# Attention blended five steps to four with the gate projections, 22 dense matmuls taken from the second RWKV inverse, 20 put between the third quarter's masks, and the merge released behind them

## The chip, the cores and the metric

One core of a Trainium2 chip runs the whole layer in one launch. The metric is the device time of that launch in microseconds; lower is better. TensorE (PE) does the matmuls and the 128x128 transposes, VectorE (DVE) and ScalarE (ACT) the elementwise work, GpSimd (POOL) a few powers and some DMA issues, and the SyncE queue (SP) issues most DMAs, in order.

## The reference

A decoder layer over 1024 tokens of width 1024, in float32. What matters here:

```python
p_rwkv, p_att, p_idx, p_gate = jnp.split(rmsnorm(h, norm1_g) @ w_in, c, axis=-1)
y_a = rwkv7_mix(token_shift(p_rwkv, tshift_mu), ...)      # a scan over tokens, 8 heads of 64x64 state
y_b = dsa_attention(q, k, v, q_idx, k_idx, w_idx)         # each query attends to its 256 best keys
g_a, g_b = jnp.split(jax.nn.sigmoid(p_gate), 2, axis=-1)
merged = g_a * (y_a @ w_o_rwkv) + g_b * (y_b @ w_o_att)
h = h + merged @ w_out
z_gate, z_up = jnp.split(rmsnorm(h, norm2_g) @ w_ffn_in, 2, axis=-1)
h = h + (jax.nn.silu(z_gate) * z_up) @ w_ffn_out
return rmsnorm(h, normf_g)
```

## The kernel before

The tokens are two halves of 512 (half 0 and half 1). Every dense projection is three matmul passes per 128x128 weight tile (`mm3`, lines 142, 143 and 147): weights and activations are split into a rounded high part and a remainder, and high x high, high x low and low x high are added up in one PSUM bank `acc`, 24 matmuls of 128x512 for an inner width of 1024. These are the **dense** matmuls below. Everything else of TensorE goes through five PSUM banks called `mix`.

RWKV is worked in four **quarters** of 256 tokens (`q` = 0 to 3; the page's quarter names below are "first" to "fourth"), two in each call of `rwkv`. A quarter has a chain of small steps that can't be dense: the decay matmuls (line 573), the norms of k (sums at line 603, transposes at 626, a power on POOL, transposes at 638, spreading at 646), the **masks** (line 701: for each of four chunks eight small matmuls of B/K against A/R into two `mix` banks, which DVE multiplies with a causal mask into `MT`, line 705, and whose diagonal blocks SP stores to `d_n`, line 712), the transposes of B/K into `NAT` (line 720), the **inverse** of 64 triangular 32x32 blocks (SP loads `N` from `d_n`, line 730; DVE runs 31 steps, lines 739 and 741; SP stores `d_w` and loads `TT`, lines 743 and 752; DVE transposes `TZ`, line 755), and then the chunk steps, which begin at line 769.

Between these steps PE is given other work from a queue `fill` of generators. Each generator issues a few matmuls and yields how many; `pump(n)` adds n credits and draws from the queue until they are used up, and `ticks(n, m)` does it in m portions, with one step of a top-k search beside each. PE's instructions run in exactly the order in which the code issues them; on the other engines and in the DMA queues a scheduler sets the order. In the first three quarters the queue holds: v's projection, the gates of half 0, and then `att0`, which draws 16 steps of the gates of half 1 and then blends the attention of half 0 with the rest of these gates.

A step of a gate yields 4 matmuls. An attention unit (head pair and query block) is five steps: logits of one head (line 1097), transposes of the unit before (line 1132), the same for the second head, and the values of the unit before that (line 1142); a finished head pair has its sums spread (line 1157). The logits are biased and reduced on DVE (line 1099) and made exponentials on ACT (line 1102); the transposes are copied out by ACT (line 1134).

`ready` is called once, in the third quarter. It draws everything that is left in the queue, gives the memory of attention and of the activations of half 1 (`u1hi`, `u1lo`) free, and begins the **merge** of half 0: SP loads the two branches' outputs, 8 tiles of 128x512 (line 1267), into `ylo`, ACT rounds each into `yhi` (line 116) and DVE takes the difference (line 117). `ylo` and `yhi` lie where `u1lo` and `u1hi` lay, so the loads wait for the last matmul that reads `u1lo`, the rounding for the last that reads `u1hi`. Then the merge's dense matmuls and the feed-forward of half 0 are the fill of the rest of RWKV.

Of the kernel before, what the change touches and what calls it, by code (L numbers as in the profile page):

```python
# [51 lines left out]
def block_kernel(ctx: ExitStack, tc: tile.TileContext, ins: dict, outT: bass.AP, outR: bass.AP, stop=None, dbg=None):  # L52
# [56 lines left out]
    def mix():  # L109
        return psM.tile([128, HT], F32, tag="mix", name="mix")  # L110
# [66 lines left out]
    def pump(n):  # L177

        credit[0] += n
        while credit[0] > 0 and fill:  # L180
            try:
                credit[0] -= abs(next(fill[0]))
            except StopIteration:
                fill.popleft()
        if not fill:
            credit[0] = 0
# [3 lines left out]
    def ticks(n, m):  # L190

        for i in range(m):
            pump(n * (i + 1) // m - n * i // m)
            next(beside[0], None)

    def run(*gens):
        for g in gens:
            for _ in g:
                pass
# [7 lines left out]
    def blend(a, b, n, m):  # L207

        a, b = iter(a), iter(b)
        while a is not None or b is not None:  # L210
            for _ in range(n):
                if a is not None:
                    y = next(a, None)
                    if y is None:
                        a = None
                    else:
                        yield y
            for _ in range(m):
                if b is not None:
                    y = next(b, None)  # L220
                    if y is None:
                        b = None
                    else:
                        yield y
# [6 lines left out]
    def opened(side, name, **kw):  # L231
        stack = ExitStack()
        return stack, stack.enter_context(tc.tile_pool(name=name, bufs=1, side=side, reuse_waits="tile", **kw))
# [272 lines left out]
    def proj_gates(half, u, tiles):  # L506
        for g in tiles:

            def out(_, ps):
                t = tmp()  # L510
                V.tensor_tensor(t, ps, rows[half], op=ALU.mult)
                A.activation(t, t, AF.Tanh, scale=0.5)
                A.dma_start(d_g[half][g], t)

            yield from proj(CT_GA + g, [u], out)
# [27 lines left out]
    def rwkv(half, p, consts, ready=None):  # L543
# [5 lines left out]
        for q in range(2 * half, 2 * half + 2):  # L549
# [135 lines left out]
            for e in range(2):  # L685
                SY.dma_start(d_bs[q][e], bs[e::32, :])

            if q == 2:
                ready()


            MT = []
            for c in range(4):
                pr, pa = divmod(c, 2)
                m = p.tile([128, 8, 128], F32, tag=f"x{c}", name="MT")
                pss = [mix(), mix()]
                for hh in range(4):
                    for g in range(2):
                        h = 2 * hh + g
                        ct, ro = h // 2, slice((h % 2) * 64, (h % 2) * 64 + 64)  # L700
                        T.matmul(pss[g][:, hh * 128:(hh + 1) * 128],
                                 BK[ct // 2][ro, ct % 2, pr, 2 * pa:2 * pa + 2, :].rearrange("p s t -> p (s t)"),
                                 AR[ro, ct, c, :, :].rearrange("p s t -> p (s t)"), start=True, stop=True)
                for g in range(2):
                    V.tensor_tensor(m[:, g::2, :], pss[g].rearrange("p (h t) -> p h t", h=4),
                                    cmask[:, 64 - 64 * pa:192 - 64 * pa].unsqueeze(1).to_broadcast([128, 4, 128]),
                                    op=ALU.mult)
                MT.append(m)
                ba = 64 - 64 * pa
                for b in range(2):  # L710
                    i0 = (c * 2 + b) * 8
                    SY.dma_start(d_n[q][i0:i0 + 8].rearrange("h s t -> s h t"),
                                 m[ba + 32 * b:ba + 32 * b + 32, :, ba + 32 * b:ba + 32 * b + 32])
            NAT = []
            for pr in range(2):
                n = p.tile([128, 2, 512], F32, tag=f"x{4 + pr}", name="NAT")
                for pa in range(2):
                    ps = mix()
                    for ct in range(4):
                        T.transpose(ps[:, ct * 128:(ct + 1) * 128],  # L720
                                    BK[ct // 2][:, ct % 2, pr, 2 * pa:2 * pa + 2, :].rearrange("p s t -> p (s t)"),
                                    ident)
                    A.activation(n[:, pa, :], ps, AF.Copy)
                NAT.append(n)

# [32 lines left out]
                             d_bs[q][e].rearrange("c s -> (c s)").partition_broadcast(64))  # L760
            bon = v
            G.tensor_tensor(bon, v, bsp, op=ALU.mult)
            ticks((211, 236, 281, 232)[q], (13, 4, 10, 6)[q])
            both = [(h, pa, 64 - 64 * pa, 64 * pa) for h in range(8) for pa in range(2)]
            hd = [(h, h // 2, slice((h % 2) * 64, (h % 2) * 64 + 64), slice(h * 64, h * 64 + 64)) for h in range(8)]
            for pr in range(2):
# [54 lines left out]
            for pr in range(2):  # L821
                yb = p.tile([128, 2, 512], F32, tag=("P", "x6")[pr], name="yb")
                yc, y2 = yb[:, 0, :], yb[:, 1, :]
                for pa in range(2):
# [35 lines left out]
                    for h, ct, ro, hc in hd:  # L860
                        pp = at[ct % 2][0]
                        T.matmul(ps[ro, ct * 64:ct * 64 + 64], NAT[pr][:, pp, hc], UV[pr][:, pp, hc],
                                 start=True, stop=True)
# [45 lines left out]
    def masks(bp, p):  # L909

        caus = p.tile([128, 128], F32, name="caus")
        bias, kept = {}, {}
        for b in range(8):
            n = (b + 1) * 128
            if b in LATE:
                kept[b] = bp.tile([128, n], F32, name=f"kept{b}")
                bias[b] = kept[b].bitcast(BF16)[:, 0:n]
            else:
                bias[b] = bp.tile([128, n], BF16, name=f"bias{b}")
            if b < 2:  # L920
                V.memset(bias[b], 0.0)
        bp.tile([128, 16], F32, name="edge")
        return caus, bias, kept
# [560 lines left out]
    def ffn(half, zp, zs, kept):  # L1484

        for gi in range(len(GROUPS)):
            f = act_tiles(zp, "f", ("s2", "s0"))
            yield from ffn_in(f, zs, gi)
            if gi < len(GROUPS) - 1:
                yield from ffn_out(half, zp, f, gi)  # L1490
        kept.append(f)
# [165 lines left out]
    def chain(*gens):  # L1657
        for g in gens:
            yield from g
# [10 lines left out]
    caus, bias, kept = masks(bp, cp2)  # L1670
# [33 lines left out]
    at0 = []  # L1704

    def att0():
        spj.close()
        su.pop().close()
        at0.append(opened("right", "at0"))
        gates = proj_gates(1, us[1], range(16))  # L1710
        for _ in range(16):
            yield next(gates)
        yield from blend(attend(0, at0[0][1], bias), gates, 2, 2)

    fill.append(att0())
    rwkv(0, rp, consts)
    zps, z0, f0 = [], [], []

    def ready():

        run(*fill)
        fill.clear()
        at0[0][0].close()
        su.pop().close()
        zps.append(opened("left", "zp0"))
        m = merge(0, zps[0][1], z0)
        next(m)
        fill.append(chain(m, ffn(0, zps[0][1], z0, f0)))

    rwkv(1, rp, consts, ready)  # L1730
    wq[0] = SY
    sz0, zp0 = zps[0]
# [114 lines left out]
```

## Time and profile before

| | us |
|---|---|
| runs | 1724.02, 1715.69, 1714.16 |
| median | 1715.69 |
| profiled execution | 1717.53 |
| its span in the trace | 1715.5 |
| PE busy | 1686.8 (98% of the span) |
| DVE, ACT, POOL busy | 1187.7, 893.5, 94.8 |

A row of a timeline gives start, length, engine, line, operation, output and input, count, and in brackets the idle time before it with what ended it. In the count a matmul of two plain float32 operands that the code issues once may stand as two, so the 32 mask matmuls of a quarter are 64 there. A row of the stages gives the length of the stretch, then for PE, PE's weight loads, DVE, ACT and POOL the busy time, then the granted clock of TensorE (1.00 is full speed), the DMA engines' share and GB/s.

### The profile page before, as it was taken

The numbers are of one execution on the slowest core, as the hardware profiler recorded it, in microseconds if no ns is written. First come the engines' busy times: TensorE is split into PE (matmuls) and PEld (weight loads), VectorE is DVE, ScalarE is ACT, GpSimd is POOL, SyncE is SP. The second block draws the span as 40 slices with busy tenths as digits, with TensorE's granted clock in tenths as the row PEclk, the third lists the DMA queues.
The fourth block names the chain that finished last, engine by engine and source line by source line (L and its number), as shares of the span: only waits on it lengthen the run. The fifth ranks groups of instructions, "written<-read, shape, count | busy, mean of one in ns | idle before, by whom it ended". The sixth has DMA issues, their size and how long they took to land.

```text
span 1715.5 us, 28185 instructions
## 1 busy us (share of the span) xinstructions
PE 1686.8 (98%) x10748; PEld 1417.2 (83%) x10748; DVE 1187.7 (69%) x2314; ACT 893.5 (52%) x1720; POOL 94.8 (6%) x107
## 2 busy tenths in 40 slices
PE   8999999999999998999999999999999999999998
PEld 6888888878778776878787888878888899899998
DVE  6789989966467558867885655535564896686763
ACT  6365898453544688755324365533323454353442
POOL 0000000000021110000100110000000000000002
PEclk9999999999999999999999999999999999999999
DMA  5452334446357625663342633245456344635532
GB/s 214 161 153 86 99 107 151 135 114 168 104 166 209 179 90 161 193 190 109 92 123 88 232 117 120 73 155 173 138 187 182 115 156 137 183 91 148 168 112 99
DMA packets 141944, 243.58 MB, mean 142 GB/s; under 512 B 48833, under 2 KB 71041, under 8 KB 141681
## 3 DMA queue, kind: packets, MB, share of 16 engines
q1 hardware_dynamic: 119072, 170.76, 32.6%
q10 hardware_dynamic: 16128, 48.60, 9.1%
q0 software_dynamic: 6608, 22.42, 4.3%
q8 instruction: 85, 1.39, 0.3%
q14 instruction: 51, 0.41, 0.1%
HBM read 188.73 MB, written 53.00 MB: 141 GB/s over the span
## 4 chain that ended last, share of the span: by engine, by line
PE 62%; DVE 4%; ACT 2%; issue 1%; DMA 1%; POOL 1%; SPq 0%; ACTq 0%; POOLq 0%; DVEq 0%
PE acc L142 13%; PE acc L147 12%; PE acc L143 12%; PE acc L160 3%; PE mix L1557 2%; PE mix L1555 2%; PE mix L1554 2%; PE mix L1142 2%; PE mix L1132 2%; PE mix L1116 1%; PE acc L1557 1%; PE acc L1554 1%; PE acc L1555 1%; DVE wlo L117 1%; PE mix L831 1%
## 5 line engine op out<-in xcount | busy, mean ns | idle before, releaser
L117 DVE TENSOR_TENSOR wlo<-wst,whi 128x1024 fp32r<-128x1024 f32 (+1 forms) x204 | 248.2, 1218 | 179.3 <-PE acc L147 71.6
L116 ACT ACTIVATE whi<-wst 128x1024 fp32r<-128x1024 f32 (+1 forms) x204 | 213.4, 1048 | 187.4 <-PE acc L143 134.4
L142 PE MATMUL acc<-zhi,whi 128*128 128x512 f32 x416 | 165.6, 398 | 0.0
L143 PE MATMUL acc<-zlo,whi 128*128 128x512 f32 x416 | 162.8, 391 | 0.0
L142 PE MATMUL acc<-u1hi,whi 128*128 128x512 f32 x320 | 127.9, 400 | 0.0
L143 PE MATMUL acc<-u1lo,whi 128*128 128x512 f32 x320 | 125.0, 391 | 0.0
L142 PE MATMUL acc<-u0hi,whi 128*128 128x512 f32 (+1 forms) x320 | 123.3, 388 | 0.0
L143 PE MATMUL acc<-u0lo,whi 128*128 128x512 f32 (+1 forms) x320 | 121.7, 383 | 0.0
L147 PE MATMUL acc<-zhi,wlo 128*128 128x512 f32 x416 | 107.7, 396 | 0.0
L142 PEld LDWEIGHTS acc<-zhi,whi 128*128 128x128 f32 x416 | 78.4, 189 | 17.6 <-issue 1.8
L142 PE MATMUL acc<-fhi,whi 128*128 128x512 f32 x234 | 91.9, 393 | 0.6 <-ACT whi L116 0.5
L143 PEld LDWEIGHTS acc<-zlo,whi 128*128 128x128 f32 x416 | 78.5, 189 | 15.4
L143 PE MATMUL acc<-flo,whi 128*128 128x512 f32 x234 | 91.1, 389 | 0.0
L147 PEld LDWEIGHTS acc<-zhi,wlo 128*128 128x128 f32 x416 | 77.2, 189 | 16.5 <-issue 1.2
L147 PE MATMUL acc<-u1hi,wlo 128*128 128x512 f32 x320 | 81.8, 395 | 0.0
L147 PE MATMUL acc<-u0hi,wlo 128*128 128x512 f32 (+1 forms) x320 | 79.4, 387 | 0.0
L996 ACT ACTIVATE junkl<-kept,z 128x1024 int8<-128x1024 int16 (+1 forms) x64 | 69.4, 1084 | 4.7 <-DVE kept L965 4.4
L142 PEld LDWEIGHTS acc<-u1hi,whi 128*128 128x128 f32 x320 | 60.1, 188 | 12.5 <-issue 0.9
L142 PEld LDWEIGHTS acc<-u0hi,whi 128*128 128x128 f32 x320 | 60.4, 189 | 11.9 <-issue 0.4
L143 PEld LDWEIGHTS acc<-u0lo,whi 128*128 128x128 f32 x320 | 60.5, 189 | 11.0
L143 PEld LDWEIGHTS acc<-u1lo,whi 128*128 128x128 f32 x320 | 60.2, 188 | 11.3
L147 PEld LDWEIGHTS acc<-u1hi,wlo 128*128 128x128 f32 x320 | 58.9, 188 | 12.6 <-issue 0.9
(447 smaller groups left out, 4000.8 us busy)
## 6 DMA issues: line engine op xcount, KB each, us to landing
wst<-in_w_ffn_in SPq DMA_DIRECT2D x72, 512.0 KB, 4.1
wst<-in_w_in ACTq DMA_DIRECT2D x36, 512.0 KB, 5.3
wst<-in_w_in SPq DMA_DIRECT2D x27, 512.0 KB, 4.0
wst<-in_w_fo SPq DMA_DIRECT2D x25, 512.0 KB, 3.6
h<-in_xT SPq DMA_DIRECT2D x32, 256.0 KB, 5.2
d_g<-tmp ACTq DMA_DIRECT2D x32, 256.0 KB, 3.2
k<-d_k POOLq DMA_DIRECT2D x16, 512.0 KB, 5.7
tmp<-d_g SPq DMA_DIRECT2D x32, 256.0 KB, 3.5
```

Of the source, the lines that this page charges most:

```text
L116: A.activation(hi, x, AF.Copy)
L117: V.tensor_tensor(lo, x, hi.bitcast(F32), op=ALU.subtract)
L142: T.matmul(ps, whi[:, wk + k, :], ahi[:, ak + k, tok], start=k == 0, stop=False)
L143: T.matmul(ps, whi[:, wk + k, :], alo[:, ak + k, tok], start=False, stop=False)
L147: T.matmul(ps, wlo[:, wk + k, :], ahi[:, ak + k, tok], start=False, stop=k == nk - 1)
L160: T.matmul(ps, w[:, k, :], a[:, k, tok], start=k == 0 and j == 0, stop=k == nk - 1 and j == 2)
L996: A.activation(junka[:, :n], y, AF.Sign, bias=z[:, i:i + 1], accum_out=cnt[:, i:i + 1])
L1132: T.transpose(ps[:, j * 128:(j + 1) * 128], L[:, (c + j) * 128:(c + j + 1) * 128], ident)
L1142: T.matmul(py[64 * e:64 * e + 64, bi * 128:(bi + 1) * 128], v[:, j, 64 * e:64 * e + 64], pts[e][j // 4][:, j % 4, :], start=j == b, stop=j ...
L1554: T.matmul(ps, whi[:, k, :], ahi[:, k, :], start=opens and k == 0, stop=False, skip_group_check=True)
L1555: T.matmul(ps, whi[:, k, :], alo[:, k, :], start=False, stop=False, skip_group_check=True)
L1557: T.matmul(ps, wlo[:, k, :], ahi[:, k, :], start=False, stop=k == 3, skip_group_check=True)
```

## The change

Four edits, all in what is drawn when. The blend of attention and gates goes from two steps and two to five and four, so that a whole attention unit is issued in one piece and 16 dense matmuls follow. The second quarter's inverse is covered by 214 credits and not 236. In the third quarter each of the four mask chunks is followed by `pump(5)`. And `ready` is called behind the transposes into `NAT`, not ahead of the masks.

```diff
             for e in range(2):
                 SY.dma_start(d_bs[q][e], bs[e::32, :])
-            if q == 2:
-                ready()
             MT = []
             for c in range(4):
...
                     SY.dma_start(d_n[q][i0:i0 + 8].rearrange("h s t -> s h t"),
                                  m[ba + 32 * b:ba + 32 * b + 32, :, ba + 32 * b:ba + 32 * b + 32])
+                if q == 2:
+                    pump(5)
             NAT = []
...
                 NAT.append(n)
+            if q == 2:
+                ready()
...
-            ticks((211, 236, 281, 232)[q], (13, 4, 10, 6)[q])
+            ticks((211, 214, 281, 232)[q], (13, 4, 10, 6)[q])
...
-        yield from blend(attend(0, at0[0][1], bias), gates, 2, 2)
+        yield from blend(attend(0, at0[0][1], bias), gates, 5, 4)
```

In the changed file the masks stand at line 697 (before 701), the stores of `d_n` at 708 (712), `NAT` at 718 (720), and everything from line 727 on one line later. The text goes by the numbers of before.

PE around the third quarter's masks, before. `u1hi` and `u1lo` are the activations of half 1 that the gates read, `AR` and `BK` the operands of the masks, `yhi` the merge's.

```order
L1142 MATMUL mix<-pt,v 64x128 x14
L147 MATMUL acc<-u1hi,wlo 128x512 x8
L1157 MATMUL mix<-kc,ri 64x128 x8
L603 MATMUL mix<-x_6780,ind 32x256 x4
L701 MATMUL mix<-AR,BK 128x128 x32
L720 MATMUL mix<-kc,BK 128x128 x16
L142 MATMUL acc<-yhi,whi 128x512
L143 MATMUL acc<-ylo,whi 128x512
```

The same place after the change, from the last of the four mask chunks on.

```order
L697 MATMUL mix<-AR,BK 128x128 x8
L142 MATMUL acc<-u1hi,whi 128x512
L143 MATMUL acc<-u1lo,whi 128x512
L142 MATMUL acc<-u1hi,whi 128x512
L143 MATMUL acc<-u1lo,whi 128x512
L147 MATMUL acc<-u1hi,wlo 128x512 x4
L718 MATMUL mix<-kc,BK 128x128 x16
L147 MATMUL acc<-u1hi,wlo 128x512 x4
L142 MATMUL acc<-yhi,whi 128x512
```

Between attention's last values (line 1142) and the merge's first matmul stood 8 dense matmuls, and now stand 80; four of them are behind each mask chunk, and the last four on `u1hi` stand directly ahead of the merge's first.

The SP queue at the same place, before: `d_bs` are the bonus sums, `ylo` the merge's loads, `P` a broadcast of the sums, `d_g` the stored gates.

```order
L1267 DMA ylo<-d_ya_111 128x512 x4
L1267 DMA ylo<-d_yb_113 128x512 x2
L686 DMA d_bs_118<-bs 4x256 x2
L1179 DMA d_yb_113<-tmp 128x512
L1267 DMA ylo<-d_yb_113 128x512
L712 DMA d_n_122<-MT 32x8x32 x2
L1267 DMA ylo<-d_yb_113 128x512
L759 DMA P<-d_bs_118 64x1024
L712 DMA d_n_122<-MT 32x8x32 x4
```

And after it.

```order
L686 DMA d_bs_118<-bs 4x256 x2
L708 DMA d_n_122<-MT 32x8x32 x2
L760 DMA P<-d_bs_118 64x1024
L708 DMA d_n_122<-MT 32x8x32 x4
L760 DMA P<-d_bs_118 64x1024
L708 DMA d_n_122<-MT 32x8x32 x2
L554 DMA wa<-d_rw_95 128x256
L1268 DMA ylo<-d_ya_111 128x512 x4
L1268 DMA ylo<-d_yb_113 128x512 x4
L731 DMA N<-d_n_122 64x1024 x2
```

The eight loads of `ylo` moved from ahead of the stores of `d_n` to behind them and behind a load of the fourth quarter (`wa`), and the load of `N` for the inverse now stands directly behind them.

PE in attention, during the second quarter's inverse, before: `k,q` are logits, `kc,L` transposes, `pt,v` values.

```order
L1142 MATMUL mix<-pt,v 64x128 x8
L147 MATMUL acc<-u1hi,wlo 128x512 x8
L1097 MATMUL mix<-k,q 128x384 x2
L1132 MATMUL mix<-kc,L 128x128 x2
L142 MATMUL acc<-u1hi,whi 128x512
L143 MATMUL acc<-u1lo,whi 128x512
```

And the same unit after it.

```order
L147 MATMUL acc<-u1hi,wlo 128x512 x8
L1143 MATMUL mix<-pt,v 64x128 x8
L1098 MATMUL mix<-k,q 128x384 x2
L1133 MATMUL mix<-kc,L 128x128 x2
L1098 MATMUL mix<-k,q 128x384 x2
L1133 MATMUL mix<-kc,L 128x128 x2
L142 MATMUL acc<-u1hi,whi 128x512
```

Where eight dense matmuls stood after every second step of attention, logits and transposes of both heads now follow one another, and 16 dense matmuls come behind.

## The prediction, made before the changed kernel was timed

> **What bounds the kernel now.** First the page: busy times, then the chain that ended last.
>
> ```profile
> span 1715.5 us, 28185 instructions
> ...
> PE 62%; DVE 4%; ACT 2%; issue 1%; DMA 1%; POOL 1%; SPq 0%; ACTq 0%; POOLq 0%; DVEq 0%
> ```
>
> The chain runs over PE; the page's table of busy times, in the section on the profile, has PE at 1686.8 us of 1715.5. The change removes no matmul and adds none. It can only win or lose in the 28.7 us in which PE has nothing, in stretches at a lower clock, and in small losses where PE goes from one kind of matmul to another. So the stages come next (length; busy PE, weight loads, DVE, ACT, POOL; clock; DMA).
>
> ```profile
> 575.00:600.00 25.00, 23.74 (x320) 18.42 (x321) 12.58 (x33) 19.59 (x50) 1.97 (x3) 1.00 0.62 187
> 600.00:625.00 25.00, 23.74 (x312) 18.96 (x313) 15.67 (x39) 22.71 (x61) 2.89 (x3) 1.00 0.25 78
> 625.00:650.00 25.00, 23.28 (x144) 18.38 (x143) 13.69 (x35) 20.20 (x57) 1.66 (x1) 1.00 0.42 132
> ...
> 670.00:686.00 16.00, 12.01 (x104) 10.14 (x99) 12.64 (x21) 14.07 (x33) 0.34 (x1) 0.79 0.68 195
> ```
>
> The reader is to see where the edits work: 4.2 us of idle PE (75 less 23.74, 23.74 and 23.28) in the second quarter's chunk steps and the third's start, and 4.0 us at the third quarter's masks, where the clock is 0.79 too. 17 us, which would be 1% (about the least that a measurement of this kernel tells from no change), are not there to be had.
>
> **The masks: 7.5 us less.** PE's timeline there:
>
> ```profile
> 669.25 1.09 PE L1157 MATMUL mix<-kc,ri 128*64 128x128 f32 x16
> 670.27 0.64 PE L603 MATMUL mix<-x,ind 128*32 128x256 f32 x8
> 670.84 1.16 PE L701 MATMUL mix<-AR,BK 64*128 64x128 f32 x16
> 672.78 2.88 PE L701 MATMUL mix<-AR,BK 64*128 64x128 f32 x34 [0.78 <-DVE MT L705]
> 676.37 1.16 PE L701 MATMUL mix<-AR,BK 64*128 64x128 f32 x14 [0.71 <-DVE MT L705]
> 679.98 3.67 PE L720 MATMUL mix<-kc,BK 128*128 128x128 f32 x16 [2.45 <-DVE MT L705]
> 683.31 0.78 PE L142 MATMUL acc<-yhi,whi 128*128 128x512 f32 x1
> ...
> 685.50 0.39 PE L143 MATMUL acc<-ylo,whi 128*128 128x512 f32 x1
> ```
>
> From the first mask to the merge are 12.5 us (683.31 less 670.84). DVE says why PE waited:
>
> ```profile
> 675.64 0.68 DVE L705 TENSOR_TENSOR MT<-mix,cmask 128x512 f32<-128x512 f32 x1
> 676.24 3.08 DVE L117 TENSOR_TENSOR ylo<-ylo,yhi 128x512 fp32r<-128x512 f32 x5
> 679.25 2.47 DVE L705 TENSOR_TENSOR MT<-mix,cmask 128x512 f32<-128x512 f32 x4
> ```
>
> The merge's differences stand between the mask products, which free the five banks. The first quarter shows the same work without them:
>
> ```profile
> 376.05 4.29 PE L701 MATMUL mix<-AR,BK 64*128 64x128 f32 x64
> 380.27 1.97 PE L720 MATMUL mix<-kc,BK 128*128 128x128 f32 x16
> 382.07 0.60 PE L473 MATMUL mix<-kc,tmp 128*128 128x128 f32 x4
> ```
>
> That is 6.0 us (382.07 less 376.05), so 6.5 were lost. The granted clock was halved besides:
>
> ```profile
> 680.00:682.00 2.00, 2.00 (x10) 2.00 (x11) 2.00 (x4) 2.00 (x5) 0.00 (x0) 0.50 0.24 43
> ```
>
> It cost the merge's first five matmuls 1.0 us more (2.2 us from 683.31 to 685.50, against 5 x 0.23; for 0.23 see below). With the change all eight differences stand behind the masks, and a chunk gives DVE two products of 0.61 us while PE has 1.06 us of masks (4.22 over 4) and 0.92 us of dense matmuls (4 x 0.23): nothing waits. The 20 dense matmuls are only moved. I take the whole 7.5 us; 5 if the gates' own work on DVE (a weight split and a scaling) still holds a bank once or twice.
>
> **The merge: 3.5 us more, and 0.7 for the clock.** Ahead of the merge the cover is now thin. Its loads wait for the last read of `u1lo`, and stand on SP behind the stores of the masks.
>
> ```profile
> 665.63 1.76 SPq L1267 DMA_DIRECT2D ylo<-d_ya  x4
> ...
> 682.95 0.81 SPq L712 DMA_DIRECT2D d_n<-MT  x2
> ...
> DMA to landing us min/median/max: 4.0/4.0/4.0
> ```
>
> The last row is the landing of the `ylo` loads. Count from e, the end of the last mask matmul. DVE's two products end at e+1.3, two stores take 0.8, `wa` 0.4, so the first load is issued at e+2.5 and lands 4.0 later, at e+6.5. ACT rounds in about 0.6 and DVE's difference takes 0.68: `yhi` at e+7.1, `ylo` at e+7.8. PE has 8 dense matmuls, 16 transposes (1.8, from the rows above) and 4 dense until then: e+4.6. So it waits 2.5 us at its first matmul and 0.5 at the second; then the differences, 0.6 apart, stay just behind the pairs of matmuls (0.46 each), and it is 3.5 us late when the eighth pair is through. The loads themselves may be slower: 2.1 MB at 195 GB/s, the rate of 670 to 686, are 10.8 us, and then the eighth difference is ready at e+14.6 and PE 6 late. Range 3 to 6; it can't be below, as the loads can't start before the release. I take 3.5, the value that goes by the loads' own landing row; before, the five differences ran without a gap. Before, this time was hidden behind the masks: that is the price of the move.
>
> The wait of 2.5 us behind 1.8 us of transposes resembles the 2.45 us before line 720, which came with the half clock. Half of a 3.4 us stretch is 1.7; part of it passes in the wait, and it may not happen: 0.7, range 0 to 1.7. The Trainium skill, "TensorE: Matmul & The Clock Gate", section "What's actually happening", says that the clock is halved after at least one idle window of about 3.4 us; the trace has it halved after three waits none of which is that long. By that rule the 0.7 would be 0 and the sum 1712.7. Its "Part 4: PE-mode transpose" says that transposes don't count as busy; then 4.3 us would count as idle, the price would be 1.7 and the sum 1714.4.
>
> **Fewer changes of side: 2.0 us less.** Going into dense matmuls costs a little:
>
> ```profile
> 658.84 0.50 PE L142 MATMUL acc<-u1hi,whi 128*128 128x512 f32 x1
> 659.18 0.39 PE L143 MATMUL acc<-u1lo,whi 128*128 128x512 f32 x1
> 659.41 0.40 PE L142 MATMUL acc<-u1hi,whi 128*128 128x512 f32 x1
> ```
>
> The first takes 0.34 us to the next, the others 0.23: 0.11. From attention's first logits to the third quarter's `NAT` the order of before changes between dense and other matmuls 90 times, that of the change 64 times: 13 entries fewer, 1.4 us; at most as much again for leaving, where some rows show the same step and some none. I take 2.0, range 1.4 to 2.8.
>
> **The second inverse: 0.5 us more.** Its last transpose on DVE, and PE's first matmul that needs it:
>
> ```profile
> 576.10 0.43 DVE L755 STREAM_TRANSPOSE TZ<-TT 32x256 f32<-32x256 f32 x1 [0.94 <-DMA TT<-d_w]
> 576.47 0.64 DVE L1099 CUSTOM_DVE_ANT_0 L<-mix,bias 128x512 f32<-128x512 f32 x1
> ...
> 582.58 1.20 PE L769 MATMUL mix<-TZ,MT 32*32 32x32 f32 x64
> ```
>
> There are 6.0 us of cover (582.58 less 576.53). In the order 152 dense matmuls stood between line 720 and 769, now 136: 3.7 us less, and a further 1.0 from fewer changes of side. DVE's loop gets two more logits of 0.6 us (the row between) in between. 6.0 - 4.7 - 1.2 leaves 0.1: I take 0.5, range 0 to 3.
>
> **The third quarter's norms: 1.0 us more.** From line 626 to 638 runs a chain over DVE, POOL, ACT and DVE, most of it the power on POOL:
>
> ```profile
> 655.76 0.38 PE L626 MATMUL mix<-kc,nq 128*128 128x128 f32 x2
> ...
> 660.79 0.38 PE L638 MATMUL mix<-kc,nr 128*16 128x128 f32 x2
> ```
>
> It took 5.0 us without a wait. PE will have 12 dense matmuls (2.8) and a spreading of 1.0 in between (670.27 less 669.25, above), 3.9 with the changes of side: 1.1 is uncovered. I take 1.0, range 0 to 2.
>
> **Attention in bursts: 1.5 us more.** Logits and transposes wait for each other's banks where nothing dense lies between:
>
> ```profile
> PE mix L1132 <- DVE mx L1099: 0.7, 1, 0.7
> PE mix L1132 <- ACT pt L1134: 0.4, 1, 0.4
> PE mix L1097 <- ACT TT L793: 0.4, 1, 0.4
> PE mix L1132 <- ACT x L581: 0.3, 1, 0.3
> ```
>
> 1.8 us in 575 to 665. Before, transposes follow logits directly 16 times and logits transposes 6 times, now 28 and 14. At the same rate 20 more neighbours cost 1.6. Below: the third quarter's start, where 1.7 us of the idle time above lay (625 to 650), gets less of attention, so 2 us less than nothing is possible. Above: 6, if each of the 14 full bursts waits for a bank about 0.4 us.
>
> **The third inverse: nothing.** Its `N` now loads behind eight `ylo` loads, and its cover was 0.3 us.
>
> ```profile
> 696.85 0.18 DVE L739 TENSOR_TENSOR tw<-W,N 128x31 f32<-128x31 f32 x1
> ...
> 744.88 0.90 DVE L755 STREAM_TRANSPOSE TZ<-TT 32x256 f32<-32x256 f32 x2 [1.97 <-DMA TT<-d_w]
> 746.04 1.20 PE L769 MATMUL mix<-TZ,MT 32*32 32x32 f32 x64
> ```
>
> But its loop began 16.9 us after the first transpose of line 720, behind the merge's first epilogues; now DVE has it directly behind the differences, some 11 us after. PE meanwhile comes 4 us later, for its wait at the merge. Range 0 to 2.
>
> **Sum.** -7.5 + 3.5 + 0.7 - 2.0 + 0.5 + 1.0 + 1.5 = -2.3 us. The profiled execution took 1717.53 us, 2.0 more than its span and 1.8 more than the median of the runs; -2.3 on the span of 1715.5 is 1713.2, and on the median of 1715.69 it is **1713.4**.
>
> **The rivals.** (1) Slower: the merge waits for its loads. Place: its first eight pairs of matmuls. At the 142 GB/s that the page gives as the mean, 2.1 MB take 14.8 us, the eighth difference is ready at e+18.6, PE 10 late, and the sum is +4.2: 1719.9. It decides from a wait of 5.8 us on. For it: the release comes only some 4 us of PE work ahead of the merge, and the merge's weights and `N` load at the same time. Against: 142 GB/s is a mean over stages that ask for little, and the stage itself moved 195. (2) The bursts wait for banks: 6 us in place of 1.5, 1717.9. For it: four of the five banks are taken in one burst, the fifth holds the values, and RWKV wants two. Against: at least 16 dense matmuls (3.7 us) now lie between bursts, and a bank is free after 0.6 us of DVE or ACT. (3) All covers hold: attention 2 us less, norms, inverse and clock nothing, merge 3.0, changes 2.8: -9.3, 1706.4. (4) That the credits go elsewhere than to the masks: the order printed above shows them there, no chance.
>
> **How the numbers follow.** Forecast 0.50 (1709 to 1717), rival 1 0.20, rival 2 0.12, rival 3 0.16, others 0.02. The range goes from just under rival 3 to just over rival 1: 1705 to 1721. Faster by over 1% means under 1698.5, slower 1732.8; no case reaches either: 0.02 and 0.03, and 0.95 for within.
>
> **What would show it.** In the changed profile: no wait of line 701's and 720's matmuls on `MT`; a wait of 2 to 4 us of the first matmul on `yhi`, released by ACT's rounding; one of about 1 us at the third quarter's line 638; at most one at the second's 769; idle PE from 575 to 650 not below 3 us. I am wrong if the merge starts without a wait (then faster), or if the chunk steps of the second quarter show a wait at each logits.

## The result, and the profile after

The changed kernel takes **1735.2 us** (median of five runs, 1731.7 to 1737.3), against 1715.6 us for five of the kernel before: a ratio of **1.0097, 95% interval 1.0080 to 1.0114** (taken over the runs, so it is not the quotient of the two medians, 1.0114). The forecast was 1713.4 us, with a range of 1705 to 1721. The change makes the kernel slower by 1%: 1735.2 lies above the 1732.8 us for which the prediction gave a chance of 0.03.

The page first, of the profiled execution (1735.7 us).

```profile
span 1733.6 us, 28189 instructions
...
PE 1693.9 (98%) x10748; PEld 1420.3 (82%) x10748; DVE 1187.9 (69%) x2314; ACT 893.7 (52%) x1720; POOL 94.0 (5%) x107
```

The span is 18.1 us longer. PE is busy 7.1 us longer with the same 10748 matmuls (1693.9 against 1686.8), so some of them ran slower; the other 11 us are idle time. DVE and ACT do the same work in the same time. The stages show where (length; busy PE, weight loads, DVE, ACT, POOL; clock; DMA):

```profile
575.00:600.00 25.00, 22.64 (x299) 17.82 (x298) 12.35 (x30) 18.65 (x49) 1.96 (x3) 0.86 0.39 101
650.00:675.00 25.00, 21.26 (x128) 15.75 (x126) 18.89 (x36) 18.44 (x38) 2.90 (x1) 0.93 0.19 64
675.00:700.00 25.00, 20.75 (x135) 15.68 (x135) 15.69 (x22) 20.79 (x50) 2.37 (x1) 0.86 0.73 216
860.00:885.00 25.00, 25.00 (x117) 21.28 (x116) 17.04 (x43) 7.28 (x10) 2.40 (x1) 0.90 0.35 94
```

Before, 575 to 600 had a clock of 1.00 and 23.74 us of busy PE, and 650 to 675 had 1.00 and 24.22; 675 to 700 had 0.86 and 21.79 already then. Now clock and busy time fall together in the second quarter's chunk steps and at the third quarter's start, and the clock falls behind the fourth quarter's masks too. PE's waits (total, times, longest), by the changed file's line numbers:

```profile
PE acc L408 <- ACT u0hi L281: 6.7, 1, 6.7
PE acc L142 <- ACT yhi L116: 4.3, 1, 4.3
PE mix L1143 <- ACT pt L1135: 3.1, 1, 3.1
PE mix L1133 <- DVE mx L1100: 2.5, 3, 1.3
PE mix L638 <- DVE nr L117: 2.2, 3, 1.1
PE mix L770 <- DVE mx L1100: 1.7, 1, 1.7
PE mix L697 <- DVE MT L701: 1.7, 1, 1.7
```

The first row is at the kernel's start and was 6.6 us before. Gone are the waits on `MT` at the third quarter's masks (3.9 us before; the row of `L697` here is the fourth quarter's). New are the merge's on `yhi`, the attention values' on their copies `pt`, and those of attention's transposes and of RWKV's line 770 on banks that the logits' reduction on DVE (`mx`) frees.

**The budget.** A wait is not the only way to lose time, so each matmul of a trace is put into an account. From the trace of before I took, for each pair of neighbouring kinds of matmul, the mean time from one start to the next, without waits and at full clock. With these pitches the order of any kernel of this case gives a time without a wait; each matmul's real start then says whether the rest is a wait (over 0.25 us too late), the price of a halved clock (late inside a halved stretch), or small change. Before, the 1701.7 us from the first matmul's start to the last's are 1676.6 of order, 21.3 of waits, 5.6 of halved clock and -1.9 of rest. The table gives the difference from that, in us, from the profiled run of each kernel that bears on the blend; the ratio is that of the runs, to before on the same chip, and a profiled run can lie some microseconds off its median.

| kernel | ratio, 95% interval | matmuls' span | order | waits | half clock | rest |
|---|---|---|---|---|---|---|
| changed | 1.0097 (1.0080 to 1.0114) | +17.9 | -2.0 | +11.8 | +6.0 | +2.2 |
| e1 blend alone | 1.0102 (1.0078 to 1.0127) | +22.6 | -1.8 | +16.2 | +7.4 | +1.0 |
| e2 214 alone | 1.0069 (1.0043 to 1.0094) | +13.4 | -1.7 | +9.7 | +4.2 | +1.4 |
| e3 release alone | 1.0029 (1.0016 to 1.0042) | +4.4 | -0.1 | +3.7 | +1.7 | -0.8 |
| e4 changed, old blend | 1.0013 (1.0000 to 1.0026) | +5.0 | -1.8 | +4.9 | +0.8 | +1.2 |
| e5 5 to 4, in turn | 1.0060 (1.0038 to 1.0083) | +10.8 | -0.5 | +7.2 | +3.2 | +1.1 |
| e6 4 to 4 | 1.0086 (1.0057 to 1.0115) | +14.3 | -0.2 | +6.9 | +5.7 | +2.0 |
| e12 1 to 1 | 1.0048 (1.0029 to 1.0066) | +15.3 | -0.9 | +7.6 | +7.4 | +1.3 |
| e13 one gate step more | 1.0045 (1.0029 to 1.0061) | +8.5 | -1.5 | +4.4 | +6.8 | -1.1 |
| e14 one gate step less | 1.0054 (1.0034 to 1.0074) | +10.3 | -1.4 | +5.3 | +6.0 | +0.5 |
| e15 changed, one step more | 1.0096 (1.0077 to 1.0115) | +15.2 | -1.6 | +10.8 | +3.8 | +2.4 |

No order is dearer than before's. Nearly all that is lost is waits and halved clock, about two to one in the changed kernel. How a late matmul is shared out between wait, clock and rest is a choice of the method, good to about 1 us; the matmuls' span is not.

### The profile page after: what moved, and what is told of

Its sections match the earlier page's. It is cut to its first block, busy times and chain, and to the rows that moved or that the text cites. A ratio compares the mean times of both kernels' runs of the same rounds, so it can differ in the third digit from the quotient of the medians.

```text
span 1733.6 us, 28189 instructions
## 1 busy us (share of the span) xinstructions
PE 1693.9 (98%) x10748; PEld 1420.3 (82%) x10748; DVE 1187.9 (69%) x2314; ACT 893.7 (52%) x1720; POOL 94.0 (5%) x107
## 4 chain that ended last, share of the span: by engine, by line
PE 48%; DVE 2%; ACT 1%; DMA 0%; issue 0%; POOL 0%; POOLq 0%; DVEq 0%; ACTq 0%
PE acc L142 10%; PE acc L143 10%; PE acc L147 10%; PE acc L160 3%; PE mix L1555 2%; PE mix L1558 2%; PE mix L1556 2%; PE mix L1143 1%; PE mix L1133 1%; PE mix L1117 1%; PE acc L1558 1%; PE acc L1556 1%; PE acc L1555 1%; PE acc L1457 0%; DMA wst<-in_w_ffn_in 0%; DVE wlo L117 0%
## 5 line engine op out<-in xcount | busy, mean ns | idle before, releaser
L147 PEld LDWEIGHTS acc<-u1hi,wlo 128*128 128x128 f32 x320 | 60.0, 191 | 12.6 <-issue 0.6
```

Source lines behind the costliest of these rows:

```text
L147: T.matmul(ps, wlo[:, wk + k, :], ahi[:, ak + k, tok], start=False, stop=k == nk - 1)
```

## The experiments

**The three parts by themselves (e1 to e4).**

```diff
e1 -        yield from blend(attend(0, at0[0][1], bias), gates, 2, 2)
e1 +        yield from blend(attend(0, at0[0][1], bias), gates, 5, 4)
e2 -            ticks((211, 236, 281, 232)[q], (13, 4, 10, 6)[q])
e2 +            ticks((211, 214, 281, 232)[q], (13, 4, 10, 6)[q])
e3: pump(5) behind each mask chunk and ready() behind NAT, as in the change
e4: the changed kernel with blend(..., 2, 2)
```

> The kernel before with one edit: attention's steps and gates blended 5 to 4 in place of 2 to 2. Theory A (a whole attention unit in one go opens waits on ScalarE's and VectorE's copies, and a clock halved for 3.4 us stands behind several of them): slower by 6 to 12 us, 1722 to 1728 us, with halved stretches in the second quarter's inverse or at the third quarter's start. Theory B (the blend is harmless by itself, the loss comes from the merge's later release and from the second inverse's lost cover): 1714 to 1718 us.

> The kernel before with one edit: 214 in place of 236 over the second quarter's inverse. The 22 matmuls are then issued with the rest of the gates ahead of the third quarter's masks. Theory A: the inverse had 6.0 us of matmuls to spare over its loads, so at most the wait of the products, 0 to 2 us: 1715 to 1718 us. Theory C (this cover is what was lost: the products wait 1.7 us and the clock is halved twice behind it, 3.4 us each at half speed): slower by 4 to 6 us, 1719 to 1722 us.

> The kernel before with the blend 2 to 2 and 236 over the second inverse kept; only five gate matmuls behind each mask chunk of the third quarter, and the merge released behind the transposes of BK. Theory D (release): masks gain 4.7 us, the merge's first matmul waits 4.3 to 5.2 us for the y tiles and the clock is halved 6.8 us behind it, which costs 3.4 us more: slower by 3 to 6 us, 1718 to 1722 us. Its rival (the wait costs what it shows and no more, the masks' gain pays for it): 1713 to 1716 us.

> The changed kernel with the blend 2 to 2 as before; 214, the five matmuls between the masks and the later release are kept. Theory A: 8 to 14 us of the changed kernel's 19.6 us loss go with the blend, 1721 to 1727 us. Theory B: 1731 to 1736 us, as the changed kernel.

Measured: 1739.3, 1731.2, 1724.5 and 1721.5 us, against 1718.6 of before on that chip. The blend alone loses as much as the whole change (20.7 us by the medians, more than theory A's 6 to 12), and without it the other edits lose 0.13%: theory A names the right edit. The parts don't add up (1.0%, 0.7% and 0.3% alone). With 214 but the release at its old place (e2) the spared matmuls are drawn ahead of the masks and cover nothing, and e2 lost more than either theory gave it; only together with the release are the 214 harmless.

With 236 and the old blend no gate is left for the masks, so e3 is the bare move of `ready` in the code. Its 5.9 us lie in theory D's range, but not by theory D's reason: with no gate behind the masks PE's last matmul on `u1lo` started at 662.00, six of the eight `ylo` loads left SP from 662.4 to 665.1 us, ahead of the first mask at 667.64, and PE waited 1.2 us for `yhi` and not 4.3 to 5.2. The new waits are 2.3 us for a bank in the merge and, in the fourth quarter, 3.5 us on `nrT` (1.6 before) and 2.3 on `UV`.

e2 and e4 share one wait, and the trace of e4 tells its cause: ACT in the second inverse, then PE.

```profile
577.21 1.32 ACT L1019 ACTIVATE tmp<-kept,top 128x512 f32<-128x512 int16 x2
582.20 0.61 ACT L1019 ACTIVATE tmp<-kept,top 128x384 f32<-128x384 int16 x1 [3.67 <-DMA d_yb<-tmp]
...
583.27 2.31 PE L791 MATMUL mix<-TT,TZ 32*32 32x32 f32 x64 [3.79 <-ACT TZ L773]
```

ACT unpacks kept scores of the search into a `tmp` buffer, of which there are four; one was still being stored to `d_yb`. The copies of `TZ` stand behind that in ACT's order, and PE waits for them. Before, PE came to these matmuls at 586.06, 6.6 us later than it was ready for them here (579.48), and ACT unpacked without waiting for a store.

**What in the blend is dear (e5, e6, e12, e13, e14, e15).**

```diff
e5  + spread(..., (0, 1, 0, 1, 0, 1, 0, 1, 0)): attention 5, gates 4, taken in turn
e6  + blend(..., gates, 4, 4)
e12 + blend(..., gates, 1, 1)
e13 (on the kernel before), e15 (on the changed kernel)
-        for _ in range(16):
+        for _ in range(17):
e14
+        for _ in range(15):
```

> The kernel before with attention's steps and gates at 5 to 4, but taken in turn (one, one, one, ... and one more attention step at the end) and not five in a row. Theory A1 (the burst is what opens waits: five attention steps in a row put their ScalarE and VectorE work ahead of RWKV's): most of the 1.0% loss of the 5 to 4 blend goes, within 0.3% of before. Theory A2 (the ratio does it: attention runs ahead and the gates left over stand in other places): slower by 0.7% or more, as with the blend in bursts.

> The kernel before with the ratio of 2 to 2 kept, but four attention steps and then four gate steps in a row. Theory A1 (bursts): slower by 0.6 to 1.0%, with waits of matmuls on ScalarE's and VectorE's results in the second quarter and halved clock behind them. Theory A2 (ratio): within 0.3% of before.

> The kernel before with attention's steps and gates blended 1 to 1 in place of 2 to 2, so the ratio is kept and the bursts are halved. Theory A1 (bursts open waits, so shorter ones close some): 0 to 0.4% faster than before. Theory K (the waits come of where each step meets another engine's queue, and any other order of these steps opens about as many: 0.6 to 1.0% was lost with fewer gates per step, with longer bursts and with both): 0.3 to 0.9% slower.

> The kernel before with one gate step (four matmuls) more ahead of the blend, 17 and not 16; the blend is 2 to 2 as before. Theory K (any displacement of these steps against RWKV's opens waits): 0.3 to 0.8% slower. Theory L (shares and bursts are what costs, a displacement of one step is nothing): within 0.2% of before.

> The kernel before with one gate step fewer ahead of the blend, 15 and not 16. Theory K: 0.3 to 0.8% slower. Theory L: within 0.2% of before.

> The changed kernel with one gate step more ahead of the blend, 17 and not 16. Theory K: another time, as other waits open and close, somewhere between 1.003 and 1.013 of before, and more likely under the changed kernel's 1.0097 than over it. Theory L: 1.008 to 1.0115, as the changed kernel.

Measured: 1730.3, 1735.1, 1729.0, 1725.6, 1726.9 and 1733.9 us, with before at 1717.4 to 1719.1. Neither A1 nor A2 stands: the new share in short turns loses, the old share in long bursts loses (e6, as A1 had it), and the old share in shorter bursts loses too, where A1 had a gain. e13 and e14 tell why: **one gate step, four matmuls, drawn earlier or later costs 0.45 and 0.54%**, as theory K had it. From there on every step of attention and gates stands four matmuls away from where it stood against RWKV's. PE's waits on three lines of RWKV, before and then in e13:

```profile
PE mix L720 <- DVE MT L705: 2.5, 1, 2.5
PE mix L646 <- ACT nrT L640: 1.6, 1, 1.6
PE mix L790 <- ACT TZ L772: 0.9, 3, 0.6
```

```profile
PE mix L790 <- ACT TZ L772: 3.8, 3, 3.0
PE mix L720 <- DVE MT L705: 3.6, 1, 3.6
PE mix L646 <- ACT nrT L640: 2.4, 2, 1.6
```

No edit is at these lines, PE only comes with a different step next to it. So a displacement from an order with few waits costs about half of the blend's 1.0% without any regrouping. The other half goes beyond one step's displacement (e1 has 16.2 us of new waits, e13 and e14 4.4 and 5.3); whether the share or the bursts make it isn't settled, since e5 and e12 lose no more than e14 within their intervals. e15 gave the time of the changed kernel, which both theories allow, so K's guess that another alignment would help there failed: the waits on `yhi`, on `pt`, at line 770 and at the fourth quarter's masks are all there again (3.3, 1.8, 1.6 and 3.3 us).

What such a wait is made of, at the third quarter's start in the changed kernel: attention's last values, and ACT ahead of them.

```profile
649.50 1.22 ACT L997 ACTIVATE junkl<-kept,z 128x1024 int8<-128x1024 f32 x1
650.54 0.28 ACT L997 ACTIVATION_READ_ACCUMULATOR junkl<-kept,z 128x1 f32 x1
650.63 1.13 ACT L116 ACTIVATE whi<-wst 128x1024 fp32r<-128x1024 f32 x1
652.30 1.06 ACT L591 ACTIVATE P<-x 128x1024 f32<-128x1024 f32 x1 [0.54 <-DVE x L587]
653.27 1.03 ACT L593 ACTIVATE x<-x 128x1024 f32<-128x1024 f32 x1
654.21 1.06 ACT L1135 ACTIVATE pt<-mix 128x512 f32<-128x512 f32 x2
...
654.84 1.57 PE L1143 MATMUL mix<-pt,v 128*64 128x128 f32 x16 [3.10 <-ACT pt L1135]
656.34 3.57 PE L147 MATMUL acc<-u1hi,wlo 128*128 128x512 f32 x8
```

The copies `pt` stand behind a pass of the search, a weight's rounding and two wide steps of RWKV, 649.5 to 654.2 on ACT almost without a gap. PE waits 3.1 us, and the eight matmuls behind take 3.57 us in place of about 2: the clock is halved from 656.6 to 660.0. That halving doesn't always come with the wait: in e8, below, the same matmuls wait 3.1 us for the same copies, and the clock behind is 1.00.

**The merge's start (e7 to e10, e16).**

```diff
e7: the kernel of e4, ready() called between the masks and NAT
e8: the changed kernel, behind ready()
+                ps = acc()
+                for i in range(5):
+                    T.matmul(ps, ident, MT[0][:, 0:4, :]..., start=True, stop=True)
e10: the kernel of e4
-            SY.dma_start(t, (d_ya if j < 4 else d_yb)[half][j % 4])
+            (G if half == 0 else SY).dma_start(t, (d_ya if j < 4 else d_yb)[half][j % 4])
```

> The blend 2 to 2, 214 and the five matmuls behind each mask chunk, and the merge released behind the masks but ahead of the 16 transposes of BK, some 3.5 us of TensorE work sooner than in the changed kernel. Theory D (the y tiles' load and rounding is what the merge waits for, and the wait halves the clock): the 5 us of waits on the y tiles fall to 1 to 2 us and the 3.4 us at half clock behind them go: 4 to 5 us faster than with the release behind the transposes (1721.5 us), 1715 to 1718 us. Its rival (the transposes' copies on ScalarE then stand behind the rounding of the y tiles, and the wait only changes its place): 1720 to 1723 us.

> The changed kernel with five matmuls of 512 columns in plain float32 (their result is not used) behind the release of the merge, where TensorE waited 4.3 us for the y tiles. Theory E (the idle wait is what halves the clock): the wait is filled, the 6.8 us at half clock behind it go, and the kernel is 2 to 4 us faster than the changed one: 1731 to 1733 us. Its rival (the clock falls with the work of the microseconds around, whatever stands in the wait): the halved stretch stays and the time is 1735 to 1737 us.

> The kernel of the 2 to 2 blend with the other two edits, whose y tiles are loaded by GpSimd's queue and not SyncE's. Theory G (the y loads leave late because SyncE issues them behind the eight stores of the mask products and one of attention's, as the trace shows: 678.3 to 685.9 us): they leave up to 8 us sooner, the 5 us of waits on the y tiles fall under 2 us, and the kernel is 0.15 to 0.35% faster than with SyncE's queue (1.0013 of before), 0.998 to 1.000. Its rival (the memory of the y tiles is what they wait for, which the last gate matmuls between the masks still read): the loads leave within 2 us of where they left, 1.000 to 1.002.

Measured: e7 1.0038 (1.0022 to 1.0054), e8 1.0094 (1.0069 to 1.0120), e10 1.0021 (1.0008 to 1.0033). All three left the time where it was or made it worse (e4, from which e7 and e10 differ, has 1.0013; the changed kernel 1.0097). For e7 SP's timeline says why, of e4 first and then of e7:

```profile
678.35 0.85 SPq L1268 DMA_DIRECT2D ylo<-d_ya  x2
679.43 0.99 SPq L708 DMA_DIRECT2D d_n<-MT  x2
```

```profile
677.76 0.85 SPq L1268 DMA_DIRECT2D ylo<-d_ya  x2
678.89 0.99 SPq L708 DMA_DIRECT2D d_n<-MT  x2
```

The release came 16 transposes sooner in the code, but in both kernels the first loads stand behind the same six stores of the masks on SP, and left 1.5 us behind the start of the last masks (676.81 in e4, 676.26 in e7). Meanwhile the roundings of `yhi` now share ACT with the copies of `NAT`, and PE's wait on `yhi` grew from 3.0 to 4.2 us. On GpSimd's queue (e10) the first load did leave ten microseconds sooner (668.3 against 678.3), but the last no sooner than on SP (686.5 against 685.9); the wait on `yhi` fell to 2.4 us, and nothing was gained.

In e8 the wait was filled and the clock stayed up. PE's timeline in e8, and the stage (columns as above):

```profile
683.21 4.45 PE L728 MATMUL acc<-MT,kc 128*128 128x512 f32 x10
687.78 0.50 PE L142 MATMUL acc<-yhi,whi 128*128 128x512 f32 x1
...
698.55 0.50 PE L142 MATMUL acc<-yhi,whi 128*128 128x512 f32 x1 [1.15 <-DVE tmp L1279]
```

```profile
684.00:691.00 7.00, 6.66 (x19) 3.00 (x18) 5.79 (x8) 5.68 (x13) 0.86 (x1) 1.00 0.95 319
691.00:698.00 7.00, 6.39 (x28) 4.70 (x26) 2.86 (x9) 6.14 (x15) 0.00 (x0) 1.00 0.77 235
```

The same place in the changed kernel:

```profile
692.44 0.79 PE L142 MATMUL acc<-yhi,whi 128*128 128x512 f32 x1 [4.25 <-ACT yhi L116]
...
697.84 0.40 PE L142 MATMUL acc<-yhi,whi 128*128 128x512 f32 x1
```

```profile
692.00:697.00 5.00, 4.56 (x10) 3.34 (x11) 4.30 (x7) 3.98 (x9) 0.00 (x0) 0.50 0.94 313
```

Theory E is right about the clock: with the wait filled, the merge's first matmuls ran at 1.00 and not at 0.50. It is wrong about the time. Counted from line 718, the 36th dense matmul was 1.2 us ahead of the changed kernel's, and the 48th 0.2 us behind: the wait for a bank that VectorE frees (1.15 us, the row at 698.55) had taken it back. What bounds the first two tiles of the merge is the bank that VectorE frees, not PE's clock.

The changed kernel's 4.25 us themselves are only in part the loads'. DVE, ACT and the landing of the `ylo` loads there:

```profile
688.37 2.24 DVE L117 TENSOR_TENSOR wlo<-wst,whi 128x1024 fp32r<-128x1024 f32 x1
690.53 0.68 DVE L511 TENSOR_TENSOR tmp<-acc,row 128x512 f32<-128x512 f32 x1
...
691.24 0.63 ACT L512 ACTIVATE tmp<-tmp 128x512 f32<-128x512 f32 x1 [1.16 <-DVE tmp L511]
691.77 0.61 ACT L116 ACTIVATE yhi<-ylo 128x512 fp32r<-128x512 f32 x1
...
DMA to landing us min/median/max: 2.6/4.0/6.8
```

The first load was issued at 686.55 and landed 2.6 us later, at 689.2. Its rounding began at 691.77, since a gate's activation (line 512) stood ahead of it on ACT, and that waited for DVE, which had a weight's split (line 117) and the gate's sum (line 511) to do first. So about 2.6 us of the wait are the order on ACT and DVE.

**The rounding by itself (e9, e16).** So the other way round: leave the loads where before had them, and take only the rounding from between the mask products (e9); then the gate loads of the first tile too (e16).

```diff
e9, on the kernel before, in merge
+            if half == 1:
                 split(yhi[:, j, :], ylo[:, j, :], t)
         yield -30
+        if half == 0:
+            for j in range(8):
+                split(yhi[:, j, :], ylo[:, j, :], ylo[:, j, :].bitcast(F32))
+            yield -30
...
+            if q == 2:
+                next(fill[0])
             NAT = []
e16, on e9
+            first = tmp(), tmp()
+            for i in range(2):
+                SY.dma_start(first[i], d_g[half][8 * i])
```

> The kernel before with the y tiles' loads issued where they were, ahead of the third quarter's mask products, but their rounding on ScalarE and VectorE only behind the last mask product. Theory F (VectorE's differences of the y tiles, not the place of the release, made the mask products late; the loads need their old place in SyncE's queue): the 4.6 us of waits at the masks and the transposes go, the merge's first matmul waits 0 to 1.5 us for the rounding, and the 6.8 us at half clock behind the masks go: 0.2 to 0.45% faster than before. Its rival (the rounding then stands ahead of the merge with nothing to cover it, and the wait only changes its place): within 0.15% of before or slower.

> The kernel of the later rounding (0.9988 of before), with the first tile's two loads of the gates issued together with the y tiles' loads. Theory M (the merge's first bank is held until VectorE has multiplied it by a gate tile whose load leaves SyncE only behind the stores of the mask products and the loads of the third inverse): the wait of 3.5 us for VectorE goes and 3.4 us at half clock with it, 0.2 to 0.35% faster than without, 0.995 to 0.997. Its rival (VectorE comes to it late in any case, since a weight's split and the inverse's first steps, which wait for their own load, stand ahead in its order): within 0.1% of 0.9988.

e9 gives 1717.5 us against 1719.1: **0.9988 (0.9977 to 1.0000)**, e16 0.9989 (0.9975 to 1.0002). Both beat the changed kernel by 1%; against before e9's gain is at the edge of what can be told, and in the rival's range, not in theory F's. Counted from the first mask, e9's transposes started 3.7 us sooner, which was the masks' gain, and PE gave it back here:

```profile
PE acc L142 <- DVE tmp L1284: 3.5, 1, 3.5
```

This wait stands at the merge's second tile. e16 cut it to 1.8 us and the time did not move: the rival's number, though not by its reason, since VectorE did come sooner; in its trace the waits on `TZ` in the inverses are 2.3 us in place of 1.0. What else took the gain isn't settled.

**A bank for the unpacking (e11).** On e2, ACT's unpacking goes to a PSUM bank and not to `tmp`.

```diff
-                t = tmp()
+                t = mix() if junk is None else tmp()
```

> The kernel before with 214 over the second inverse (1.0069 of before by itself), and ScalarE's unpacking of the kept sparse scores written to a PSUM bank in place of a buffer that attention's y store still holds. Theory H (in the second inverse ScalarE waits 4.0 us for that buffer, and TensorE 4.5 us for the copies queued behind it): both waits go, the 6.8 us at half clock at 584 us too, and 4 to 8 us of the 12 us lost come back, 1.002 to 1.0045 of before. Its rival (with 22 matmuls fewer the wait finds another carrier, or the loss is elsewhere): 1.006 to 1.008.

1.0052 (1.0034 to 1.0071), against 1.0069 (1.0043 to 1.0094) without: not told apart by the times, and between the ranges of theory H and its rival. In the trace the wait on `TZ` fell from 5.1 to 0.4 us and the third quarter began 3.1 us sooner than in e2 (counted from the second quarter's transposes), so the buffer was that wait's cause; but PE then waited 2.9 us at line 769 for a bank that the unpacking held, and 5.1 us at the third quarter's `NAT`, where e2 had 5.3. The wait changed its carrier.

## Why the prediction was wrong

The step that failed is the price of attention in bursts and of the second inverse behind it: the sum had +2.0 us for the two, and together with the norms, which were right, the changed kernel lost 12.6 us there. By place, in us: what the sum had, and what the changed trace lost there beyond the pitches of its order.

| | forecast | measured |
|---|---|---|
| changes of side (the order itself) | -2.0 | -2.0 |
| second quarter's `NAT` to third's masks: attention +1.5, inverse +0.5, norms +1.0 | +3.0 | +12.6 |
| third's masks -7.5, merge's start +3.5 and clock +0.7 | -3.3 | +0.6 |
| ahead of these | 0 | -0.6 |
| third's line 769 to the end | 0 | +7.3 |

At the second inverse's line 769 (770 in the changed file) what came last was not the inverse's own chain, whose cover the prediction had counted, but a bank held for the logits' reduction:

```profile
581.03 0.76 PE L770 MATMUL mix<-TZ,MT 32*32 32x32 f32 x32 [1.70 <-DVE mx L1100]
```

- **Attention in bursts and the second inverse failed**, and they are most of the error. The burst term counted neighbours on PE at the old rate of bank waits, 1.5 us; its upper end was 6. The 12.6 us are 5.3 in the second inverse (waits at logits and transposes ahead of it, 1.7 at line 769, and a halved clock behind), 2.3 in the chunk steps, 5.5 at the values of the third quarter's start with the clock behind them, 1.0 at the norms, and -1.5 elsewhere. What was missed is that a PE row moved by a few matmuls meets other rows on ACT and DVE, which run one after another in these traces: the third quarter's start, which the prediction thought might gain 2 us, lost 5.5. e13 and e14 put the price of even one step at 0.5%. Rival 2 had the waits for banks, but not the largest loss, which is the values' wait for ACT's copies; its 6 us were too few.
- **The clock** was priced at one place, 0.7 us. There alone the merge's first twelve matmuls took 5.4 us (692.44 to 697.84) in place of 12 x 0.23, 2.6 more. Apart from the kernel's last microseconds, 27.3 us are at half clock, against 13.7 before, and they cost 6.0 us more.
- **The masks** came out as forecast in kind: no wait on `MT` is left, and 3.9 us were saved up to the first transpose of `NAT`. The rest of the 7.5 lay in the merge's first matmuls, and those are late again. e9 shows that this was no matter of the release alone: with 1.3 of the 3.9 us of waits on `MT` left, 3.5 us return at the merge's second tile.
- **The merge's wait** was 4.25 us at the first matmul, and the next ones came 0.9 late, in part by the clock: 5.1 against 3.5, inside its 3 to 6, and released by ACT's rounding as foreseen. In part that is luck: the term was made of SP's queue and the loads' landing, and the first load landed 2.6 us behind its issue and not 4.0, while the order on ACT and DVE added about 2.6 us that the term did not have. Rival 1, by slow loads, did not come: its wait of 5.8 us or more wasn't reached.
- **The norms** came out at 1.0 us as forecast, and the order's own gain at 2.0.
- **Behind the merge** the sum had nothing. The fourth quarter's masks waited 2.7 us for `BK` and `MT`, with 6.8 us at half clock behind. No edit is there; with the old blend (e4) only 1.8 us were lost in that part. About 3 of the 7.3 us came still later, behind the fourth inverse, where PE waited 1.2 us for `zlo` and 0.7 each for `zhi` and a weight `whi`. Which of the displaced steps opened these waits wasn't tried, so this part's cause stays open.

The prediction began from the 28.7 us in which PE had nothing, in which the change "can only win or lose". That bounds what can be won and not what can be lost: PE's idle time grew by 11 us. The sentence that "no case reaches" 1% slower was wrong for this reason, and because each cover was tested against the old time of its own chain. The release and the 214, the parts that I worked out most closely, cost 0.13% together.

In the changed kernel halved clock began in the wait of 4.25 us and within 1.8 us behind the waits of 1.70, 3.10 and 1.66 us; ahead of the two other stretches (434.75 and 588.35) the longest idle time in 3.41 us was 0.22 us. On the clock the Trainium skill, "TensorE: Matmul & The Clock Gate", section "What's actually happening", has the halving after at least one idle window of about 3.4 us; here even the stretch at the wait of 4.25 us began 2.6 us into it (690.75, the wait began at 688.19), so the trace doesn't bear this out as a condition. Another section of that page of the Trainium skill, "A second HAM failure mode: psum-queue depth-cycling", says that frequent short idle times between groups can throttle too; no run here tests that, since the stretch that e8 removes stood at a single long wait.

## What to carry to other kernels

Where several engines each work through interleaved streams, cover is not a quantity that can simply be moved: a change of the interleaving is priced by the waits that it opens, and those are found on ACT's and DVE's timelines at the new place, not on PE's. Try a displacement of one step first: if that already costs half a per cent, as here, the present order is likely a narrow optimum and any larger regrouping starts with that debt. A wait that is removed pays only if the next engine in line is ahead of it; look for the next wait before counting the gain.

## What the hardware showed

- The halved clock comes in stretches of 3.41, 6.83 or 10.24 us in all of these traces, apart from each kernel's first and last microseconds, and the starts within one trace lie whole multiples of 3.41 us apart (434.75, 581.52, 588.35, 656.62, 690.75 and 858.00 in the changed kernel). Some followed waits as short as 1.7 us; a wait of 3.1 us had one behind it in the changed kernel and none in e8. What decides isn't shown. Filling the wait of 4.25 us with matmuls of no use kept the clock there at 1.00 (e8).
- A halved stretch cost less than half of its length: 27.3 us of them cost 11.6 us in the changed kernel. PE also waits in them (the one that begins at 690.75 has 1.7 us of the merge's wait in it).
- One gate step, four matmuls of 0.23 us, drawn earlier cost 8 us of 1717 by displacing attention against RWKV (e13).
